# Four blocks of the first merge gate computed while the adaLN modulation is built, and the sample rows loaded as 128 contiguous half rows

## The chip, the cores and the metric

The kernel runs on one core of a Trainium2 chip. The metric is the device time of one execution in microseconds: 2131.4 us is the median of three runs of the kernel before (2131.13 to 2132.64). A core has TensorE (PE in the profile; its weight loads are PEld), VectorE (DVE), ScalarE (ACT), GpSimd (POOL) and SyncE (SP, which here issues most DMAs). They run on their own instruction streams, each in program order, and wait for each other by semaphores.

## The reference

The reference is one inference step of a one-layer hybrid decoder on 256 prompt tokens and 8 x 8 sample tokens (320 columns together), D_MODEL 2048, float32:

```
mod = silu(c) @ w_ada + b_ada;  shift, scale, gate = split(mod, 3)
h = rms_norm(x, pre_norm_g) * (1 + scale) + shift
(a_qkv, a_z, a_b, a_a, b_q, b_k, b_v, b_z, i_q, i_k, i_w, g_a, g_b) = split_columns(h @ w_in)
y_a, s_new, conv_new = gdn_branch(a_qkv, a_z, a_b, a_a, ...)      # gated DeltaNet
y_b = attend(q, k, v, i_q, i_w, i_k) * silu(b_z)                  # indexer picks top-k keys, sparse attention
merged = sigmoid(g_a) * (y_a @ w_pa) + sigmoid(g_b) * (y_b @ w_pb)
out = rms_norm(merged @ w_out, post_norm_g)
return x + gate * out, (k, v, i_k, s_new, conv_new)
```

What matters here is the first gate g_a: 2048 columns of w_in, that is 16 blocks of 128 features, each a product of a 2048 x 128 weight block with the 320 columns of h, followed by a sigmoid.

## The kernel before, in words

**The products.** Activations are kept with features on the partitions: xh and xl are a rounded high part and the rest of h, 16 blocks of 128 features by 320 tokens. A weight tile is split in the same way into whi (ACT copies it) and wlo (DVE subtracts), and a product is three matmuls: whi with xh, whi with xl, wlo with xh. A block of 128 output features over all 2048 input features takes 16 x 3 = 48 matmuls of 320 columns.

**The opening** (`startup`). h doesn't exist yet: each of its 16 feature blocks needs its shift and scale, which are columns of c @ w_ada. The opening goes in eight rounds q. In a round four tiles of w_ada of 1 MB (`columns`, four calls of eight matmuls each, fp32, listed as `pm<-raw,cT` or `rawx,cT`) give the modulation of two feature blocks; `operands` then turns the sum into columns (the `sel` matmuls, once a round), scales x and writes two blocks of xh and xl. As soon as these two blocks exist, the products that can use them run as jobs from a first-in first-out list (`fifo`, taken by `run(n)`): eight blocks of the indexer's queries (`iq_job`, EARLY = 8; 192 prompt and 64 sample columns), one block of values (`bv_job`), and five small blocks (`held_job`). The held ones keep a PSUM bank each for all rounds; the others write to a bank that is added to SBUF by DVE after each job (`add_to`) and goes back to the ring. That ring, `ps_main`, has three banks here (pm_65, pm_66, ps_72 in the listings), of which a round's `columns` hold one. The loads of a round (four tiles of w_ada, one of 1 MB for the queries, one of 0.72 MB for the small blocks) are issued by SP in the order of `seq`, as tiles of a ring of six come free. `split` makes awh and awl of the small blocks' weights; both have one buffer, so ACT can write awh only when the last held job of the round before has run.

**The stream.** Then 128-feature blocks are streamed through `stream`: two units of 24 matmuls a block, weights split two units ahead. Between the units (`side_round`) generators put in the instructions of the side work: attention of the prompt, the indexer's top-k, and `sample_branch`, which goes through eight samples b one after the other: bias and score matmuls, reductions on DVE, exponentials on ACT, transposes, copies, the product with V. A planner with a clock of its own decides at which unit a side step is put into the instruction streams. The chunks of the attention stage are, in order: the other eight query blocks, 16 blocks of b_q, 16 of b_z, 16 of g_a, and four early blocks of a_z. The next stage (DeltaNet) may only begin when every side generator has ended: `chunks[0].ready = lambda: not self.sides`. `stream` then calls `force`, which steps the side generators with no unit in between until they have all ended.

Of the kernel before, what the change touches and what calls it, by code (L numbers as in the profile page):

```python
# [17 lines left out]
NP = 256  # L18
# [17 lines left out]
EARLY = 8  # L36
AHEAD = 4
# [167 lines left out]
class Kernel:  # L205
# [210 lines left out]
    def build(self):  # L416
# [28 lines left out]
        for t in self.cst.free:  # L445
            self.nc.gpsimd.memset(t, 0.0)
# [18 lines left out]
    def consts(self):  # L465
# [6 lines left out]
        self.ident_b = self.l0.tile([128, 128], BF, name="ident_b")  # L472
        v.tensor_copy(self.ident_b, self.ident)
# [19 lines left out]
    def startup(self):  # L493
# [12 lines left out]
        awl = sp.tile([128, 2, 720], F32R, name="awl")  # L506
        seq = []
        for q in range(8):
            seq += [("a", q, 0), ("a", q, 1), ("a", 8 + q, 0), ("a", 8 + q, 1), ("i", q, 0), ("w", q, 0)]
        raws, aws, iqs = {}, {}, {}  # L510
        pos = {"n": 0}

        def load():
            while pos["n"] < len(seq):
                kind, q, h = seq[pos["n"]]
                r = awr if kind == "w" else ring
# [8 lines left out]
                elif kind == "w":  # L525
                    for d0, c0, n in ((0, C_IK, 144), (144, C_BA, 64), (208, C_BK, 512)):
                        nc.sync.dma_start(t[:, :, d0:d0 + n], w[rows, c0:c0 + n].rearrange("(k p) c -> p k c", p=128))
                    aws[q] = t
                else:
# [15 lines left out]
        for e in range(2):  # L545
            nc.scalar.dma_start(x[2][64 * e:64 * e + 64], xs[:, 1024 * e:1024 * e + 1024])
# [44 lines left out]
        both = sp.tile([128, 128], F32, name="both")  # L591
        for e in range(2):
            self.tt(both[:, 64 * e:64 * e + 64], self.ident[:, 0:64], self.ident[:, 64:128], OP.add)
# [23 lines left out]
        msb = sp.tile([128, 512], F32, name="msb")  # L617
# [14 lines left out]
        def split_i(q, g):  # L632
# [13 lines left out]
            low()  # L646

# [48 lines left out]

        def first_jobs():
# [8 lines left out]
        def jobs(q):  # L706
# [4 lines left out]
            fifo.append(lambda: bv_job(q))  # L711
            for j in range(len(held)):
                fifo.append(lambda j=j: held_job(q, j))
# [13 lines left out]
        def operands(q, turned=None):  # L727
# [3 lines left out]
            for e in range(4):  # L731
                self.mm(p[:, 9 * e:9 * e + 9], msb[:, 128 * e:128 * e + 128], self.sel)
# [16 lines left out]
        for q in range(8):  # L749
# [14 lines left out]
            if q == 1:  # L764
                run(2)
                split(0)
                run(2)
            p = self.ps_main.get()
            columns(q, 0, 0, p)
            if q == 0:  # L770
                idle_turns(14)
            columns(q, 0, 1, p)
            if q == 0:
                idle_turns(14)
            elif q == 1:
                run(4)
            else:
                split(q - 1)
                run(5)
# [3 lines left out]
            if q == 0:  # L783
# [5 lines left out]
                idle_turns(8)  # L789
            columns(q, 1, 1, p)  # L790
            self.act(msb, p)
# [4 lines left out]
            elif q > 1:  # L796
                run(4)
# [10 lines left out]
        jobs(7)  # L808
        run(5)
        split(7)  # L810
        run(4)
        self.split_ahead(1)
        run(3)
        self.split_ahead(2)
        run(2)
        self.ps_main.free.remove(self.side5)
        self.ps_side.put(self.side5)
        self.shut("start")
# [92 lines left out]
    def modulate(self, k, p, gs, mod, h):  # L911
        self.ts(h[:, :NP], p[:, :NP], gs[:, k, 0:1], mod[:, k, 0:1], OP.mult, OP.add)
        hs = h[:, NP:NT].rearrange("p (b t) -> p b t", t=TS)
        c0 = NP + 64 * (k // 8)
# [1532 lines left out]
```

## Time and profile before

| what | value |
|---|---|
| median of three runs | 2131.4 us |
| profiled execution, its own time | 2132.65 us |
| its span, first to last instruction | 2130.9 us |
| PE busy in the span | 2099.3 us (99%) |
| DVE, ACT, POOL busy | 66%, 46%, 22% |
| opening, first to last held job | until 169.6 us |
| attention stage, first to last streamed block | 169.7 to 715.7 us |
| `sample_branch`, K and V loop of eight samples | 561.9 to 715.7 us |

The page gives busy time by engine, then the span in 40 slices, then DMA queues, the chain of waits, and groups of instructions. Every operation goes through one helper, so all lines read L63 and instructions are told apart by tile names. Neighbouring matmuls overlap, so that the row of one shows 0.31 us while the next begins 0.147 us later: what a matmul costs is the distance between starts.

### The profile page before, as it was taken

The numbers are of one execution on the slowest core, as the hardware profiler recorded it, in microseconds if no ns is written. First come the engines' busy times: TensorE is split into PE (matmuls) and PEld (weight loads), VectorE is DVE, ScalarE is ACT, GpSimd is POOL, SyncE is SP. The second block draws the span as 40 slices with busy tenths as digits, with TensorE's granted clock in tenths as the row PEclk, the third lists the DMA queues.
The fourth block names the chain that finished last, engine by engine and source line by source line (L and its number), as shares of the span: only waits on it lengthen the run. The fifth ranks groups of instructions, "written<-read, shape, count | busy, mean of one in ns | idle before, by whom it ended". The sixth has DMA issues, their size and how long they took to land.

```text
span 2130.9 us, 43963 instructions
## 1 busy us (share of the span) xinstructions
PE 2099.3 (99%) x17055; PEld 2006.3 (94%) x17055; DVE 1410.9 (66%) x2881; ACT 989.6 (46%) x2257; POOL 463.1 (22%) x653
## 2 busy tenths in 40 slices
PE   7999999999999999999999999999999999999997
PEld 5889999899999999999999999999999999999997
DVE  4665657899755678868787878787746545445543
ACT  3235464333344455565656565656535424233343
POOL 2000100000001036545444444445440000000000
PEclk9999999999999999999999999999999999999999
DMA  9996656985787766777877777777787967555562
GB/s 332 355 309 173 181 151 178 289 256 151 201 238 239 205 181 173 211 210 207 207 200 199 208 196 210 193 212 192 200 218 210 268 180 218 161 155 146 166 178 85
DMA packets 720336, 438.91 MB, mean 206 GB/s; under 512 B 74144, under 2 KB 705536, under 8 KB 717824
## 3 DMA queue, kind: packets, MB, share of 16 engines
q1 hardware_dynamic: 716032, 413.45, 68.9%
q0 software_dynamic: 3616, 21.02, 3.0%
q8 instruction: 134, 2.20, 0.4%
q10 hardware_dynamic: 480, 1.65, 0.3%
q14 instruction: 74, 0.61, 0.1%
HBM read 386.81 MB, written 48.94 MB: 204 GB/s over the span
## 4 chain that ended last, share of the span: by engine, by line
PE 72%; issue 23%; DMA 2%; DVE 2%; ACT 0%; SPq 0%; DVEq 0%; POOL 0%; POOLq 0%; ACTq 0%
PE pm L63 56%; PE ps L63 16%; DMA raw<-in_w_ada_dram 1%; DVE S L63 1%; DMA rawx<-in_w_in_dram 1%; DVE wlo L63 0%; SPq L63 0%; DMA c<-in_c_sample_dram 0%; DVE awl L63 0%; DMA out_dram<-S 0%; ACT whi L63 0%; ACT ot L63 0%; DVE sga L63 0%; DVE w L63 0%; DVEq L2443 0%
## 5 line engine op out<-in xcount | busy, mean ns | idle before, releaser
L63 PE MATMUL pm<-xh,whi 128*128 128x320 f32 (+1 forms) x3284 | 996.1, 317 | 1.9 <-DVE qiS L63 0.8
L63 PE MATMUL pm<-xl,whi 128*128 128x320 f32 (+1 forms) x3284 | 962.1, 307 | 0.4 <-DVE xl L63 0.3
L63 DVE TENSOR_TENSOR wlo<-raw,whi 128x1024 fp32r<-128x1024 f32 x474 | 589.1, 1252 | 280.8 <-ACT whi L63 264.9
L63 PEld LDWEIGHTS pm<-xh,whi 128*128 128x128 f32 x3284 | 617.6, 188 | 32.2 <-issue 23.9
L63 PEld LDWEIGHTS pm<-xl,whi 128*128 128x128 f32 x3284 | 618.1, 188 | 1.7 <-DVE xl L63 0.8
L63 ACT ACTIVATE whi<-raw 128x1024 fp32r<-128x1024 f32 x474 | 497.7, 1058 | 169.7 <-PE pm L63 150.8
L63 PE MATMUL pm<-xh,wlo 128*128 128x320 f32 (+1 forms) x3284 | 547.6, 307 | 0.0
L63 PEld LDWEIGHTS pm<-xh,wlo 128*128 128x128 f32 x3284 | 495.4, 188 | 0.0
L63 POOL TENSOR_TENSOR X<-X,tmpx 48x31 f32<-48x31 f32 (+15 forms) x248 | 175.9, 709 | 19.4
L63 POOL TENSOR_TENSOR tmpx<-blk,X 48x31 f32<-48x31 f32 (+15 forms) x248 | 160.4, 647 | 51.0 <-DMA blk<-d_b 32.8
L63 PE MATMUL pm<-y1h,whi 128*128 128x320 f32 x512 | 151.3, 308 | 1.1 <-ACT y1h L63 1.1
L63 PE MATMUL pm<-y1l,whi 128*128 128x320 f32 x512 | 151.3, 307 | 0.2
L63 DVE SCALAR_TENSOR_TENSOR ps<-xp,cs,ps 128x344 f32<-128x344 f32 x192 | 111.5, 581 | 6.8
L63 POOL TENSOR_TENSOR rfin<-rfin,mh 128x3 f32<-128x3 f32 x1 | 0.8, 848 | 486.4 <-DVE rfin L63 486.4
L63 POOL TENSOR_TENSOR sc<-sc,mh 128x6 f32<-128x6 f32 (+1 forms) x24 | 43.6, 1815 | 277.0 <-DVE sc L63 213.0
L63 PEld LDWEIGHTS pm<-y1h,whi 128*128 128x128 f32 x512 | 95.7, 187 | 1.4 <-ACT y1h L63 1.3
L63 PEld LDWEIGHTS pm<-y1l,whi 128*128 128x128 f32 x512 | 96.1, 188 | 0.7 <-DVE y1l L63 0.7
L63 PE MATMUL pm<-y1h,wlo 128*128 128x320 f32 x512 | 85.4, 308 | 0.0
L63 PEld LDWEIGHTS pm<-y1h,wlo 128*128 128x128 f32 x512 | 77.7, 187 | 0.0
L63 DVE SCALAR_TENSOR_TENSOR S<-S,gtr,ps 128x128 f32<-128x128 f32 x256 | 67.4, 341 | 0.1
L63 ACT ACTIVATE xp<-pm 128x256 f32<-128x256 f32 (+1 forms) x128 | 32.0, 304 | 69.9 <-PE pm L63 69.9
L63 ACT ACTIVATE ot<-ot,sc 128x128 f32<-128x128 f32 x96 | 29.9, 390 | 72.3 <-DVE sc L63 72.3
(374 smaller groups left out, 2308.0 us busy)
## 6 DMA issues: line engine op xcount, KB each, us to landing
raw<-in_w_in_dram SPq DMA_DIRECT2D x336, 512.0 KB
raw<-in_w_pa_dram SPq DMA_DIRECT2D x64, 512.0 KB
rawx<-in_w_ada_dram SPq DMA_DIRECT2D x18, 1024.0 KB
a<-in_w_ada_dram SPq DMA_DIRECT2D x16, 1024.0 KB
S<-in_state_gdn_dram SPq DMA_DIRECT2D x32, 512.0 KB
out_dram<-S SPq DMA_DIRECT2D x32, 512.0 KB
raw<-in_w_pb_dram SPq DMA_DIRECT2D x32, 512.0 KB
raw<-in_w_out_dram SPq DMA_DIRECT2D x32, 512.0 KB
```

Of the source, the lines that this page charges most:

```text
L63: made = fn(*args, **kw)
```

## The change

Four of the sixteen g_a blocks (GATED = 4) leave the stream and become jobs of the opening. Each round loads two more row blocks of w_in by 512 columns (0.5 MB) into a single buffer gwr, listed in `seq` behind the round's other loads; `split_g` makes their high and low parts in the third pair of whi and wlo buffers; four `ga_job`s per round run 6 matmuls of 320 columns each and add the result into four SBUF tiles (two of them borrowed: auxf and vtok). In the last round the sums get their tanh, the affine step of the sigmoid, and the store to `d_siga`. In `startup` the jobs are also run in another pattern: before, the two `columns` calls of a half round stood together; now two or more jobs stand between all four. The modulation sums are evacuated into two 256-column tiles (`cst`, which the DeltaNet stage uses later, and whose clearing moves to the opening's end) in place of one of 512. A bf16 copy of the identity that nothing used is gone. The 64 sample rows of 2048 are loaded as 128 rows of 1024 (half rows, two to a token, next to each other) by one DMA in place of two, and `both` and `modulate` read them in that order.

```diff
 EARLY = 8
+GATED = 4
 AHEAD = 4
...
         self.cst = Ring([c.tile([128, 256], F32, name=f"cst{j}") for j in range(2)])
-        for t in self.cst.free:
-            self.nc.gpsimd.memset(t, 0.0)
         self.CS, self.CSV = {}, {}
...
         v.tensor_scalar(self.ident, ji, 0.0, None, op0=OP.is_equal)
-        self.ident_b = self.l0.tile([128, 128], BF, name="ident_b")
-        v.tensor_copy(self.ident_b, self.ident)
         self.ones = self.l0.tile([128, 128], F32, name="ones")
...
         awl = sp.tile([128, 2, 720], F32R, name="awl")
+        gwr = Ring([sp.tile([128, 2, 128 * GATED], F32, name="gwr")])
+        ga = [self.auxf[:, 0:NT], self.vtok.rearrange("p c d -> p (c d)")[:, 0:NT]]
+        ga += [sp.tile([128, NT], F32, name=f"ga{j}") for j in range(GATED - 2)]
         seq = []
         for q in range(8):
-            seq += [("a", q, 0), ("a", q, 1), ("a", 8 + q, 0), ("a", 8 + q, 1), ("i", q, 0), ("w", q, 0)]
-        raws, aws, iqs = {}, {}, {}
+            seq += [("a", q, 0), ("a", q, 1), ("a", 8 + q, 0), ("a", 8 + q, 1), ("i", q, 0), ("w", q, 0), ("g", q, 0)]
+        raws, aws, iqs, gws = {}, {}, {}, {}
         pos = {"n": 0}
...
                 kind, q, h = seq[pos["n"]]
-                r = awr if kind == "w" else ring
+                r = {"w": awr, "g": gwr}.get(kind, ring)
                 if not r.free:
...
                     aws[q] = t
+                elif kind == "g":
+                    nc.sync.dma_start(t, w[rows, C_GA:C_GA + 128 * GATED].rearrange("(k p) c -> p k c", p=128))
+                    gws[q] = t
                 else:
...
         xs = i["x_sample"].rearrange("b t d -> (b t) d")
-        for e in range(2):
-            nc.scalar.dma_start(x[2][64 * e:64 * e + 64], xs[:, 1024 * e:1024 * e + 1024])
+        nc.scalar.dma_start(x[2], xs.rearrange("r (e c) -> (r e) c", e=2))
         nc.scalar.dma_start(x[1], i["x_prompt"][0, 128:256, :])
...
         both = sp.tile([128, 128], F32, name="both")
+        pairs = lambda t: t.rearrange("p (r e) -> p r e", e=2)
         for e in range(2):
-            self.tt(both[:, 64 * e:64 * e + 64], self.ident[:, 0:64], self.ident[:, 64:128], OP.add)
+            self.tt(pairs(both)[:, :, e], pairs(self.ident)[:, :, 0], pairs(self.ident)[:, :, 1], OP.add)
 
...
         gs = sp.tile([128, KB, 9], F32, name="gs")
-        msb = sp.tile([128, 512], F32, name="msb")
+        msb = self.cst.free
         hT = [sp.tile([128, NT], F32, name=f"hT{j}") for j in range(2)]
...
             low()
+
+        def split_g(q):
+            r = gws.pop(q)
+            hi, lo = self.whi.get(), self.wlo.get()
+            hv, lv = (x.rearrange("p k c -> p (k c)").rearrange("p (k c) -> p k c", k=2) for x in (hi, lo))
+            halves[q, 2] = hi, lo, hv, lv
+            self.act(hv[:, :, :128 * GATED], r)
+            self.tt(lv[:, :, :128 * GATED], r, hv[:, :, :128 * GATED], OP.subtract)
+            gwr.put(r)
+            load()
 
...
 
+        def ga_job(q, j):
+            hi, lo, hv, lv = halves[q, 2]
+            p = self.ps_main.get()
+            products(q, p[:, :NT], hv, lv, 128 * j, 128, True, True)
+            add_to(q, p, [(ga[j], p[:, :NT])])
+            if j == GATED - 1:
+                self.whi.put(hi)
+                self.wlo.put(lo)
+                del halves[q, 2]
+            if q == 7:
+                t = ga[j]
+                self.act(t, t, AF.Tanh, scale=0.5)
+                self.ts(t, t, 0.5, 0.5, OP.mult, OP.add)
+                nc.sync.dma_start(self.d_siga[j], t)
+
         def first_jobs():
...
             fifo.append(lambda: bv_job(q))
+            for j in range(GATED):
+                fifo.append(lambda j=j: ga_job(q, j))
             for j in range(len(held)):
...
             for e in range(4):
-                self.mm(p[:, 9 * e:9 * e + 9], msb[:, 128 * e:128 * e + 128], self.sel)
+                self.mm(p[:, 9 * e:9 * e + 9], msb[e // 2][:, 128 * (e % 2):128 * (e % 2) + 128], self.sel)
             if q == 0:
...
                 run(2)
+            elif q > 1:
+                split(q - 1)
+                run(2)
             p = self.ps_main.get()
...
                 idle_turns(14)
+            else:
+                run(2)
+                if q == 1:
+                    split_g(0)
             columns(q, 0, 1, p)
...
             elif q == 1:
-                run(4)
+                run(2)
             else:
-                split(q - 1)
-                run(5)
+                run(3)
+                split_g(q - 1)
             if q >= AHEAD:
...
                 idle_turns(8)
+            else:
+                run(2)
             columns(q, 1, 1, p)
-            self.act(msb, p)
+            for e in range(2):
+                self.act(msb[e], p[:, 256 * e:256 * e + 256])
             self.ps_main.put(p)
...
                 idle_turns(5)
-            elif q > 1:
-                run(4)
+            else:
+                run(1 if q == 1 else 4)
             if q in then:
...
         jobs(7)
+        split(7)
         run(5)
-        split(7)
+        split_g(7)
         run(4)
         self.split_ahead(1)
-        run(3)
+        run(4)
         self.split_ahead(2)
-        run(2)
+        run(5)
         self.ps_main.free.remove(self.side5)
         self.ps_side.put(self.side5)
+        for t in self.cst.free:
+            nc.gpsimd.memset(t, 0.0)
         self.shut("start")
...
         hs = h[:, NP:NT].rearrange("p (b t) -> p b t", t=TS)
-        c0 = NP + 64 * (k // 8)
         bc = lambda a: a[:, k, 1:9].rearrange("p (b o) -> p b o", o=1).to_broadcast([128, NB, TS])
-        self.tt(hs, p[:, c0:c0 + 64].rearrange("p (b t) -> p b t", t=TS), bc(gs), OP.mult)
+        self.tt(hs, p[:, NP:384].rearrange("p (b t e) -> p e b t", t=TS, e=2)[:, k // 8], bc(gs), OP.mult)
         self.tt(hs, hs, bc(mod), OP.add)
...
         chunks += self.pairs(w, C_BZ, 16, self.bz_done, r)
-        ga = self.pairs(w, C_GA, 16, lambda p, h: self.gate_done(p, h, self.d_siga, self.t_r), r)
+        ga = self.pairs(w, C_GA + 128 * GATED, 16 - GATED,
+                        lambda p, h: self.gate_done(p, GATED + h, self.d_siga, self.t_r), r)
         ga[0].before = lambda: self.spawn(self.conv_gen(0))
```

The first place where instructions move is PE's stream in the fifth round of the opening (q = 4), behind the last of the held jobs that the round begins with (ps_71 is its accumulator). Before:

```order
L63 MATMUL ps_71<-xh,awl 128x320 x2
L63 MATMUL pm_65<-rawx_165,cT 32x256 x8
L63 MATMUL pm_65<-raw_75,cT 32x256 x8
L63 MATMUL pm_66<-xh,whi_78 128x256
L63 MATMUL pm_66<-xl,whi_78 128x256
L63 MATMUL pm_66<-xh,whi_78 128x256
```

and with the change:

```order
L64 MATMUL ps_72<-xh,whi_78 128x256
L64 MATMUL ps_72<-xl,whi_78 128x256
L64 MATMUL ps_72<-xh,whi_78 128x256
L64 MATMUL ps_72<-xl,whi_78 128x256
L64 MATMUL ps_72<-xh,wlo_81 128x256 x2
L64 MATMUL pm_66<-xh,whi_78 128x256
L64 MATMUL pm_66<-xl,whi_78 128x256
L64 MATMUL pm_66<-xh,whi_78 128x256
L64 MATMUL pm_66<-xl,whi_78 128x256
L64 MATMUL pm_66<-xh,wlo_81 128x256 x2
L64 MATMUL pm_65<-rawx_161,cT 32x256 x8
L64 MATMUL ps_72<-xh,whi_78 128x256
```

Two query jobs have moved ahead of the first `columns`, and the third job (last row, bank ps_72 again) follows it where the second `columns` stood. On DVE the subtraction of awl still stands ahead of the additions that free these banks; with the change, in the same round:

```order
L64 TENSOR_TENSOR awl<-awr_163,awh 128x1440
L64 TENSOR_TENSOR q_137<-ps_72,q_137 128x192
L64 TENSOR_TENSOR qiS<-ps_72,qiS 128x8x8
L64 TENSOR_TENSOR q_138<-pm_66,q_138 128x192
L64 TENSOR_TENSOR qiS<-pm_66,qiS 128x8x8
```

The second place is PE at the sixth sample of `sample_branch` (its product with V is the row `a,a`, `vS` belongs to it; `esel` and `bs` are the bias matmuls of the next sample). Before, with the units of the stream around it:

```order
L63 MATMUL ps_67<-a_1770,a_1773 64x128 x16
L63 MATMUL ps_67<-vS,a_1773 64x128 x2
L63 MATMUL pm_66<-xh,whi_78 128x320
L63 MATMUL pm_66<-xl,whi_78 128x320
```

and with the change:

```order
L64 MATMUL ps_69<-a_2038,a_2039 64x128 x16
L64 MATMUL ps_69<-vS,a_2039 64x128 x2
L64 LDWEIGHTS esel
L64 MATMUL ps_67<-bs,esel 128x256
L64 LDWEIGHTS esel
L64 MATMUL ps_70<-bs,esel 128x256
```

From here on no matmul of the stream follows until the eighth sample is done; the next one stands here:

```order
L64 MATMUL ps_69<-a_2036,a_2039 64x128 x16
L64 MATMUL ps_69<-vS,a_2039 64x128 x2
L64 MATMUL ps_71<-ident,a_2040 128x128
L64 MATMUL pm_65<-xh,whi_79 128x320
L64 MATMUL pm_65<-xl,whi_79 128x320
```

Before, 168 matmuls of the stream stand between the sixth sample's product with V and the end of the eighth; with the change none does. The stream has 192 fewer to place.

The third place is SP's queue for the opening's second round (q = 1), where the new load stands between the small blocks' weights and the first tile of w_ada of the next round. Before:

```order
L63 DMA awr_167<-in_w_in_dram 128x2x512
L63 DMA raw_76<-in_w_ada_dram 128x8x256
```

and with the change:

```order
L64 DMA awr_163<-in_w_in_dram 128x2x512
L64 DMA gwr<-in_w_in_dram 128x2x512
L64 DMA raw_76<-in_w_ada_dram 128x8x256
```

What is behind gwr on SP waits until `split_g` has emptied that one buffer.

## Prediction

> **What bounds the kernel now.** I read the page first, then the waits of PE, then single stretches of the timeline. Busy time by engine and the share of it in 40 slices (a digit is tenths):
>
> ```profile
> span 2130.9 us, 43963 instructions
> PE 2099.3 (99%) x17055; PEld 2006.3 (94%) x17055; DVE 1410.9 (66%) x2881; ACT 989.6 (46%) x2257; POOL 463.1 (22%) x653
> ...
> PE   7999999999999999999999999999999999999997
> ```
>
> PE works all the time; 31.6 us of the span are without it. Work that moves from one place on PE to another is worth nothing by itself: the change can only win where PE waits in the opening, and it loses wherever the removed work was cover for something else. So two questions decide: how much PE waits in the opening, and what stood behind the four blocks in the stream.
>
> The waits of PE from 30 to 171 us (total, times, longest):
>
> ```profile
> PE pm L63 <- DMA raw<-in_w_ada_dram: 2.2, 2, 1.8
> PE pm L63 <- DVE qiS L63: 2.0, 4, 1.2
> PE pm L63 <- ACT msb L63: 0.7, 1, 0.7
> ```
>
> The rounds can be told by the `sel` matmuls, eight listed rows once a round; the first, two neighbours, and the eighth:
>
> ```profile
> 27.12 1.06 PE L63 MATMUL pm<-sel,msb 128*128 128x9 f32 x8
> ...
> 100.22 1.06 PE L63 MATMUL ps<-sel,msb 128*128 128x9 f32 x8
> ...
> 117.36 1.06 PE L63 MATMUL pm<-sel,msb 128*128 128x9 f32 x8
> ...
> 151.74 1.06 PE L63 MATMUL pm<-sel,msb 128*128 128x9 f32 x8
> ```
>
> Seven rounds take 124.6 us. A round without a wait takes 17.14 (100.22 to 117.36), seven of them 120.0: only 4.6 us of waits are there to be filled. DMA is as full as PE in this stretch (30 to 150 us):
>
> ```profile
> DMA packets 38358, 42.40 MB, mean 353 GB/s; under 512 B 3003, under 2 KB 34761, under 8 KB 38345
> ```
>
> That is 6.05 MB in 17.1 us; opening rounds are bound by both at once.
>
> **The change part by part.**
>
> *The work that moves.* A matmul of 320 columns costs the distance between starts; these two rows are 12 matmuls apart:
>
> ```profile
> 689.68 0.31 PE L63 MATMUL pm<-xh,whi 128*128 128x320 f32 x1
> ...
> 691.44 0.31 PE L63 MATMUL pm<-xh,whi 128*128 128x320 f32 x1
> ```
>
> 0.147 us. Four blocks are 192 matmuls, 28.2 us less in the stream; the opening gets the same 192, 3.5 us a round for eight rounds. The moved loads: 0.52 MB more a round, 6.57 MB at 353 GB/s is 18.6 us, against 17.14 + 3.5 = 20.7 us of PE. From the second or third round on PE is the later one, so the DMA waits of 2.2 us go. The single gwr holds back the next round's w_ada tiles on SP until mid round; they then have about 15 us of PE work ahead of them and their first tile needs (0.5 + 1) MB, under 5 us: hidden. If that cover were gone, every us would be paid seven times. The split of the new weights (ACT, DVE) and the additions (DVE) lie beside PE, which has 3.5 us of work for them each round; where they get in its way is the third part.
>
> *What the four blocks covered.* After the change nothing of the stream is left beside the last samples of `sample_branch`; the DeltaNet stage waits for them. One sample's chain, from its predecessor's product with V on, all engines:
>
> ```profile
> 676.68 1.97 PE L63 MATMUL ps<-a,a 128*64 128x128 f32 x32
> ...
> 678.93 0.94 POOL L63 DMA_INDIRECT a<-in_cache_k_dram,idx  x1 [14.30 <-PE ps L63]
> ...
> 680.90 0.31 PE L63 MATMUL ps<-bs,esel 32*128 32x256 bf16 x5
> ...
> 683.12 1.42 DVE L63 TENSOR_REDUCE st<-ps 128x1 f32<-128x256 f32 x4 [1.10 <-PE ps L63]
> ...
> 684.77 0.32 ACT L63 ACTIVATE a<-ps,st 128x64 f32<-128x64 f32 x1 [4.35 <-DVE st L63]
> ...
> 686.78 0.22 ACT L63 ACTIVATION_READ_ACCUMULATOR a<-ps,st 128x1 f32 x1
> ...
> 688.19 2.37 DVE L63 STREAM_TRANSPOSE a<-a 128x1024 f32<-128x1024 f32 x2
> ...
> 688.63 0.92 PE L63 MATMUL ps<-ident,a 32*128 32x32 f32 x33
> ...
> 691.78 0.93 DVE L63 COPY a<-ps 128x256 f32<-128x256 f32 x3
> ...
> 715.74 0.39 PE L63 MATMUL pm<-xh,whi 128*128 128x320 f32 x1
> ```
>
> The last row is the first matmul of the DeltaNet stage. The gather's time to landing is in the view of tile a (min/median/max):
>
> ```profile
> DMA to landing us min/median/max: 7.6/8.1/9.7
> ```
>
> Today the stretch from 676.68 (sixth sample's product with V) to 715.74 takes 39.1 us: 168 stream matmuls, 24.7, and 14.4 of the samples' own PE work. There is no slack: the samples end where the stream does. Uncovered, I add the chain: product with V 2.3 (to 678.93); seventh sample's bias and scores 2.2; maxima 1.65; exponentials 2.2, at 8.4. The next K, asked for at 2.3, lands 8.1 later, at 10.4; DVE's transposes 2.4 and, queued behind them, its copies 0.9 end at 13.7; product with V 2.3, at 16. The eighth: 2.2 + 1.65 + 2.2, PE transposes 0.9, copies 1.0, product 2.3, output 0.6, at 26.9; with some 0.1 us at each of six handovers 27.5. Another 24 matmuls (3.5 us) are gone just ahead. So the attention stage gets shorter by 39.1 - 27.5 + 3.5 = 15.1 us, and not by 28.2: **+13.1 us**. Bounds: with no wait for K 25.9, with the slowest gather 29.1, so +11.5 to +14.7.
>
> *The new pattern in the opening.* Two `columns` calls together, one alone, and the border between them and the jobs:
>
> ```profile
> 52.86 1.07 PE L63 MATMUL pm<-raw,cT 128*32 128x256 f32 x16 [1.84 <-DMA raw<-in_w_ada_dram]
> 53.86 0.38 PE L63 MATMUL pm<-xh,whi 128*128 128x256 f32 x1
> ```
>
> ```profile
> 105.27 0.45 PE L63 MATMUL ps<-xh,awl 128*128 128x320 f32 x2
> 105.52 1.40 ACT L63 ACTIVATE awh<-awr 128x1440 fp32r<-128x1440 f32 x1 [0.46 <-ACT whi L63]
> 105.65 1.93 PE L63 MATMUL ps<-rawx,cT 128*32 128x256 f32 x32
> ...
> 106.95 1.66 DVE L63 TENSOR_TENSOR awl<-awr,awh 128x1440 fp32r<-128x1440 f32 x1 [0.64 <-ACT awh L63]
> 107.52 0.39 PE L63 MATMUL pm<-xh,whi 128*128 128x256 f32 x1
> 107.74 0.28 PE L63 MATMUL pm<-xl,whi 128*128 128x256 f32 x1
> 107.86 0.28 PE L63 MATMUL pm<-xh,whi 128*128 128x256 f32 x1
> ...
> 108.54 0.36 DVE L63 TENSOR_TENSOR q<-pm,q 128x192 f32<-128x192 f32 x1
> 108.81 0.21 DVE L63 TENSOR_TENSOR qiS<-pm,qiS 128x64 f32<-128x64 f32 x1
> ...
> 109.08 0.39 PE L63 MATMUL pm<-xh,whi 128*128 128x256 f32 x1
> ```
>
> One call alone lasts 1.00 (52.86 to 53.86), two together 1.87 (105.65 to 107.52). The first job matmul behind them takes 0.22 in place of 0.12, the two ahead 0.38 in place of 0.29. Two calls apart cost 2 x 1.00 - 1.87 + 0.19 = 0.32 us more than together. The change parts both pairs in seven rounds: 14 x 0.32 = **+4.5 us**.
>
> Then the banks. awl of a round starts when ACT has awh, and ACT waits for the last held job (105.52); DVE has awl at 108.6 and only then frees the banks of the first query jobs: the third starts at 109.08, at the very moment its bank is free. Two `columns` calls now fill that time. With the change the first two jobs (0.72 each) and one call (1.2 with its borders) end at 108.3, and the third job stands 0.8 us for its bank. It and everything behind it on PE wait. In rounds 2 to 4 both halves of the query weights are split ahead of awl, and PE waits there already today (0.4 to 0.5 each of the 2.0 us above): 1.2. In round 1 the one call taken out of the way costs 0.5. Together 3 x 0.8 + 3 x 1.2 + 0.5 = **+6.5 us**; nothing if I have misread the bank (lower bound), 9 if DVE's added split delays more.
>
> *The rest.* In the opening's tail the wait for awl only moves from one job to another, and the tanh chain on ACT and DVE ends beside the held jobs, 4.4 us of PE: I take +0.5 for its start. Two evacuations for one are covered by the four gate jobs, in round 0 +0.1. The sample rows: the same 512 KB of 4 KB pieces; PE's first work waits for w_ada, not for them: 0, between -0.5 and +0.5. The clearing of `cst` and the dropped identity stood at a time when PE had nothing to do: 0.
>
> *Sum.* +13.1 - 4.6 + 4.5 + 6.5 + 0.6 = **+20.1 us**. On the profiled execution: span 2130.9 + 20.1 = 2151.0, and 1.75 around it (2132.65 against its span) is 2152.8; this execution lies 1.25 over the median of the runs, so **2151.5 us**.
>
> **The rivals.**
>
> *A: only the lost cover counts.* The banks come free in time and PE doesn't notice the new pattern: +13.1 + 0.6, with 4.6 gained or lost, 2140 to 2149, say 2145. For it, DVE is busy for 13 of 20 us only (the columns are PE, PEld, DVE, ACT, POOL, clock, DMA share, GB/s):
>
> ```profile
> 100.00:120.00 20.00, 20.00 (x185) 17.29 (x184) 13.06 (x40) 5.02 (x7) 0.00 (x0) 1.00 1.09 356
> ```
>
> Against it, awl's place in DVE's order hasn't moved.
>
> *B: PE's clock falls in the uncovered stretch.* The chain above leaves PE idle three times for about 4 us (for the seventh sample's softmax, its copies, the eighth's softmax). At the end of the trace the granted clock falls soon after PE stops:
>
> ```profile
> 2118.00:2121.00 3.00, 1.29 (x11) 1.03 (x11) 1.34 (x3) 0.62 (x4) 0.85 (x1) 0.96 0.00 0
> 2121.00:2131.00 10.00, 0.00 (x0) 0.00 (x0) 5.11 (x5) 0.00 (x0) 0.00 (x0) 0.50 0.73 262
> ```
>
> (The column ahead of the last two is the clock, 1.00 elsewhere.) If it falls in each gap, PE's 8 us behind them on the chain take up to twice as long, less what recovers, and the stream's first matmuls too: +5 to +9, 2158. The Trainium skill, "TensorE: Matmul & The Clock Gate", section "HAM oscillation — how this bites in real kernels", warns of PE-idle gaps over about 3.4 us; by its free-running windows a gap of 4 us holds a whole one only now and then. The trace agrees that the clock halves (0.50); that 4 us are enough no row here shows, so it stays a rival.
>
> *C: faster.* PE's rows overlap, so busy may hide slack; if the opening's rounds go by bytes alone, they grow by 0.52 MB each, 1.5 us, 12 in all, and with 15.1 saved in the stream the kernel is 3 us faster: 2128. It decides from the point at which the opening grows by less than 15.1 us. Against it: from 100 to 150 us starts follow each other without a wait, 17.14 us of PE in a round of 17.14. The Trainium skill, "Perfetto Trace Analysis", section "Identifying the Most-Contended Engine", holds matmul busy to be no good measure and LDWEIGHTS busy the better one; by it PE would have 2.7 of 20 us to spare here (17.29). But the fp32 calls load only 32 columns each, which lowers that share without any pause.
>
> *D: the one gwr starves PE.* Loads start late in each round and PE waits at `columns`: 2 us a round, +14 more, 2166. Against it: 15 us of lead.
>
> **How the numbers follow.** The sum 0.57, A 0.17, B 0.16, C 0.06, D 0.04. The time is that of the sum, 2151.5. The range reaches into A below (no bank waits, cheap handovers: 2140) and B above (2163). A difference under 0.2%, 4.3 us, can't be told from none. Faster by more has half of C, 0.03; the same the rest of C and a little of A, 0.05; slower 0.92.
>
> **What would show it.** The attention stage should end with some 27 us in which PE is half busy and no `whi` row stands (five tenths in the windows); in the opening, rounds of about 22 us in place of 17.14, DMA below full, and a PE wait on DVE qiS of about 1 us in each. Wrong would be: no such stretch, rounds under 20.7, or waits on gwr or w_ada from the third round on.

## The result, and the profile after

2151.3 us, the median of four runs (2151.05 to 2153.7), against 2131.8 before (2131.13 to 2132.64): a ratio of 1.0093, with a 95% interval from 1.0079 to 1.0107. The change makes the kernel slower by 19.5 us; 20.1 were forecast. The head of the page after:

```profile
span 2149.7 us, 44005 instructions
...
PE 2108.1 (98%) x17055; PEld 2010.5 (94%) x17055; DVE 1419.8 (66%) x2908; ACT 991.5 (46%) x2269; POOL 462.5 (22%) x653
...
PE   8999999999999899999999999999999999999997
```

PE has the same 17055 matmuls; the 8 in slice 14 of 40 (699 to 752 us) is new, in the middle of a kernel of nines. To see where 18.8 us of span come from I cut both traces at the same two instructions: the first transpose of auxf on PE, which ends the opening, and the first copy of a DeltaNet block out of PSUM (xp on ACT), which ends the attention stage. Before, PE's timeline, then the view of tile xp (min/median/max in ns, then the first and the last start in us):

```profile
170.97 0.37 PE L63 MATMUL ps<-ident,auxf 80*128 80x80 f32 x3
```

```profile
L63 ACT ACTIVATE xp<-pm x34: 220/318/396, 723.1 to 890.7; 128x256 f32<-128x256 f32 x17, 128x64 f32<-128x64 f32 x17
```

After:

```profile
205.04 0.37 PE L64 MATMUL ps<-ident,auxf 80*128 80x80 f32 x3
```

```profile
L64 ACT ACTIVATE xp<-pm x30: 222/306/387, 742.8 to 886.4; 128x256 f32<-128x256 f32 x15, 128x64 f32<-128x64 f32 x15
```

The opening grows by 34.1 us for 28.2 us of work; the attention stage shrinks from 552.1 to 537.8, by 14.4 for the same 28.2; the rest of the program takes 1406.9 in place of 1407.8. The sum is 18.8.

**The opening after.** The fourth, fifth, sixth and eighth `sel` marks, and PE's waits from 28 to 210 us:

```profile
92.66 1.06 PE L64 MATMUL ps<-sel,cst 128*128 128x9 f32 x8
...
115.17 1.06 PE L64 MATMUL pm<-sel,cst 128*128 128x9 f32 x8
...
137.26 1.06 PE L64 MATMUL ps<-sel,cst 128*128 128x9 f32 x8
...
181.43 1.06 PE L64 MATMUL pm<-sel,cst 128*128 128x9 f32 x8
```

```profile
PE pm L64 <- DVE qiS L64: 5.0, 6, 1.3
PE ps L64 <- DVE qiS L64: 3.3, 4, 1.1
```

From the fourth mark on a round takes 22.1 to 22.5 us in place of 17.14. The waits for DMA are gone, and every round from the second on has one wait of 0.7 to 1.1 us on qiS; the longest, 1.3, lies in the tail behind the rounds. This is the sixth round, PE and DVE:

```profile
121.90 1.66 DVE L64 TENSOR_TENSOR awl<-awr,awh 128x1440 fp32r<-128x1440 f32 x1 [0.64 <-ACT awh L64]
...
122.03 1.07 PE L64 MATMUL pm<-rawx,cT 128*32 128x256 f32 x16
123.48 0.35 DVE L64 TENSOR_TENSOR q<-pm,q 128x192 f32<-128x192 f32 x1
123.74 0.21 DVE L64 TENSOR_TENSOR qiS<-pm,qiS 128x64 f32<-128x64 f32 x1
...
124.01 0.39 PE L64 MATMUL pm<-xh,whi 128*128 128x256 f32 x1 [0.92 <-DVE qiS L64]
```

PE has done two jobs and one `columns` call when the third job needs a bank whose addition stands behind awl on DVE.

**The uncovered stretch after.** PE's timeline from the sixth sample's product with V to the first DeltaNet matmul, then windows over the wait for the seventh sample's softmax and what follows it (the column behind the five engines is the granted clock):

```profile
707.23 1.97 PE L64 MATMUL ps<-a,a 128*64 128x128 f32 x32
...
715.65 0.92 PE L64 MATMUL ps<-ident,a 32*128 32x32 f32 x33 [3.44 <-ACT a L64]
718.86 4.02 PE L64 MATMUL ps<-a,a 128*64 128x128 f32 x32 [2.29 <-issue]
...
729.71 1.01 PE L64 MATMUL ps<-ident,a 32*128 32x32 f32 x33 [3.74 <-ACT a L64]
730.98 3.50 PE L64 MATMUL ps<-a,a 128*64 128x128 f32 x32 [0.27 <-ACT a L64]
...
735.45 0.39 PE L64 MATMUL pm<-xh,whi 128*128 128x320 f32 x1
```

```profile
712.20:715.60 3.40, 0.01 (x1) 0.00 (x0) 1.10 (x4) 2.23 (x10) 1.46 (x7) 1.00 0.98 382
715.60:718.80 3.20, 0.92 (x33) 0.69 (x33) 3.14 (x7) 0.66 (x2) 0.00 (x0) 0.68 0.52 215
718.80:722.90 4.10, 4.04 (x34) 3.65 (x36) 0.48 (x2) 0.00 (x0) 0.00 (x0) 0.50 0.01 4
```

For 28.2 us (707.23 to 735.45) there is no row of the stream. Behind each long wait for a softmax the clock is halved, and the next product with V takes 4.0 and 3.5 us. At full clock it takes 1.97, or 2.31 where no stream stands beside it (the kernel with matmuls in the gaps, below).

### The profile page after: what moved, and what is told of

It reads as the page before. It is cut to its first block, busy times and chain, and to the rows that moved or that the text cites. A ratio compares the mean times of both kernels' runs of the same rounds, so it can differ in the third digit from the quotient of the medians.

```text
span 2149.7 us, 44005 instructions
## 1 busy us (share of the span) xinstructions
PE 2108.1 (98%) x17055; PEld 2010.5 (94%) x17055; DVE 1419.8 (66%) x2908; ACT 991.5 (46%) x2269; POOL 462.5 (22%) x653
## 4 chain that ended last, share of the span: by engine, by line
PE 41%; issue 23%; DVE 2%; ACT 0%; DMA 0%; DVEq 0%; POOL 0%; POOLq 0%; SPq 0%; ACTq 0%
PE pm L64 33%; PE ps L64 8%; DVE S L64 1%; DVE wlo L64 0%; DMA out_dram<-S 0%; DVE w L64 0%; DVE ps L64 0%; ACT ot L64 0%; ACT a L64 0%; DVE sga L64 0%; DVEq L2486 0%; ACT whi L64 0%; DVE sc L64 0%; POOL sc L64 0%; DVE ot L64 0%
## 5 line engine op out<-in xcount | busy, mean ns | idle before, releaser
L64 DVE TENSOR_TENSOR wlo<-raw,whi 128x1024 fp32r<-128x1024 f32 x466 | 576.8, 1247 | 265.5 <-ACT whi L64 252.9
L64 ACT ACTIVATE whi<-raw 128x1024 fp32r<-128x1024 f32 x466 | 489.4, 1058 | 174.6 <-PE pm L64 151.4
```

Of the source, the lines that this page charges most:

```text
L64: made = fn(*args, **kw)
```

## The experiments

Each is timed beside the kernel before on the same chip. The time is the median of all executions, and ratios carry their 95% intervals; stages are cut as above, in the one execution that was profiled.

| kernel | time, us | against before | opening | attention stage | rest |
|---|---|---|---|---|---|
| before | 2131.8 to 2132.9 | 1 | 171.0 | 552.1 | 1407.8 |
| changed | 2151.3 | 1.0093 (1.0079 to 1.0107) | 205.0 | 537.8 | 1406.9 |
| additions first | 2148.1 | 1.0077 (1.0060 to 1.0094) | 199.1 | 538.7 | 1408.6 |
| columns paired | 2145.9 | 1.0069 (1.0052 to 1.0085) | 196.5 | 540.6 | 1407.9 |
| more cover | 2162.1 | 1.0143 (1.0126 to 1.0160) | 204.5 | 552.1 | 1403.7 |
| transposes in the gaps | 2150.2 | 1.0085 (1.0068 to 1.0102) | 204.6 | 537.3 | 1406.4 |
| matmuls in the gaps | 2148.3 | 1.0072 (1.0057 to 1.0088) | 204.6 | 535.3 | 1407.2 |
| paced | 2144.0 | 1.0059 (1.0043 to 1.0074) | 204.8 | 526.8 | 1408.2 |
| paired, late split, paced | 2140.9 | 1.0036 (1.0023 to 1.0050) | 202.4 | 528.3 | 1409.3 |
| paired and covered | 2130.3 | 0.9986 (0.9977 to 0.9995) | 196.8 | 523.9 | 1407.2 |
| before, rows only | 2130.5 | 0.9990 (0.9981 to 0.9999) | 169.1 | 552.1 | 1407.6 |
| before, rows in two loads | 2132.9 | 0.9999 (0.9990 to 1.0008) | 171.6 | 552.1 | 1407.8 |

The rest of the program varies between 1406.4 and 1409.3 with no edit there (more cover apart); differences of a us or two in it are not explained below.

### Bank waits: the additions first

```diff
             elif q > 1:
-                split(q - 1)
                 run(2)
+                split(q - 1)
```

> The changed kernel (2151.3 us) with one swap: in rounds 2 to 7 the first two query jobs stand ahead of the split of the small blocks' weights, so that on DVE the additions that free two banks come before the subtraction of awl. Theory of the prediction (PE waits for banks because awl stands ahead of them): the waits of PE on DVE qiS, 8.3 us in the changed kernel, fall to about 2, and the time by about 6, to 2145. In rounds 2 to 4 both halves of the query weights still stand ahead on DVE; if these are what is late there, only 3 us come back, 2148. Rival (DVE as a whole is late, awl only sets which job pays for it): the wait moves to another job, 2151.

PE's waits for banks from 28 to 210 us:

```profile
PE pm L64 <- DVE qiS L64: 1.6, 2, 1.3
PE ps L64 <- DVE qiS L64: 1.6, 2, 1.1
```

8.3 us become 3.2, those of the second round and of the tail; in the rounds from the third on none is left. The opening ends 5.9 us sooner, of which 0.4 lies ahead of the first `sel` mark (25.33 against 25.71), where the edit changes nothing; in that execution the clock came up to full at 12.4 us, in the changed kernel's at 13.6. That is about the theory's 6: the waits come from the place of awl in DVE's order, and the halves of the query weights, which still stand ahead in rounds 2 to 4, aren't what is late. The time falls by 3.2 only. Of the difference 0.9 is in the attention stage, where this execution had more halved clock (a mean of 0.77 over its uncovered stretch of 29.2 us, 0.82 in the changed kernel), and 1.7 is in the rest, unexplained.

### Partings: the columns in pairs

```diff
             elif q > 1:
                 split(q - 1)
-                run(2)
             p = self.ps_main.get()
             columns(q, 0, 0, p)
             if q == 0:
                 idle_turns(14)
-            else:
-                run(2)
-                if q == 1:
-                    split_g(0)
             columns(q, 0, 1, p)
...
             elif q == 1:
                 run(2)
+                split_g(0)
+                run(2)
             else:
-                run(3)
+                run(7)
                 split_g(q - 1)
...
-            else:
-                run(2)
             columns(q, 1, 1, p)
...
-                run(1 if q == 1 else 4)
+                run(3 if q == 1 else 6)
```

> The changed kernel with the order of the opening as it was before: the two columns calls of a half round together, all jobs behind them (7 and 6 a round), the four gate blocks still in the opening. Theory of the prediction: 14 partings of 0.32 us (4.5) and the bank waits (6.3 above those of the kernel before) both go: 10.8 less, 2140.5, rounds of about 20.7 us. Rival A' (parting costs nothing, only the waits go): 6.3 less, 2145. Rival A (the pattern is free, the banks wait in either order): 2151. Rival (together, the columns wait for their tiles again, 2.2 and 0.7 us as in the kernel before): 2143 to 2144.

The fifth and the eighth mark with the columns in pairs, and then with the additions first (columns apart); in neither does PE wait for anything in these three rounds:

```profile
110.52 1.06 PE L64 MATMUL pm<-sel,cst 128*128 128x9 f32 x8
...
172.95 1.06 PE L64 MATMUL ps<-sel,cst 128*128 128x9 f32 x8
```

```profile
111.96 1.06 PE L64 MATMUL pm<-sel,cst 128*128 128x9 f32 x8
...
175.48 1.06 PE L64 MATMUL pm<-sel,cst 128*128 128x9 f32 x8
```

A round takes 20.81 us against 21.17: a parting costs 0.18 us, and not 0.32, which makes 2.5 for fourteen. The opening ends 8.5 us before that of the changed kernel (5.9 of waits, 2.6 of partings), and not 10.8. With 20.81 a round is 3.67 longer than a quick round before (17.14), for 3.5 of added matmuls: in pairs the moved work costs its own time. The whole gained only 5.5 at the median. The attention stage is 2.8 us longer than in the changed kernel, with more halved clock again (0.77 over the stretch of 29.6 us, and 0.81 over the 8.8 behind it), and the rest 1.0. By the time alone rival A' (2145) would fit; the opening shows that it doesn't.

### Cover: four other blocks in the place of the removed ones

```diff
-EARLY_Z = (0, 4)
+EARLY_Z = (0, 4, 8, 12)
```

> The changed kernel with four more blocks of a_z (192 matmuls, 28.2 us) taken out of the DeltaNet stage and streamed at the end of the attention stage, where the four gate blocks had stood; nothing else is changed. Theory (the lost cover of the last samples is a cost of its own): the stretch from the sixth sample's product with V to the first DeltaNet matmul is covered again as in the kernel before and ends no later than the stream; of the 28.2 us moved there 14 are hidden, and the time falls by 14, to 2137.5. Rival (the blocks are cover where they stand today, too, and the DeltaNet stage waits for its chains once they are gone): about 2151, or slower. If the samples move with the stream only in part: 2140 to 2145.

The attention stage takes 552.1 us, to a tenth what it took before. It was given 28.2 us of work over the changed kernel's 537.8, and only 14.3 of them show: half of what the stream puts there is free, as the samples are paced here. But the kernel is 10.8 slower and not 13.8 faster. The rest shrinks by 3.2 for 28.2 us taken out. Waits of PE in the DeltaNet stage (760 to 1520 us), first changed, then with more cover:

```profile
PE ps L64 <- DVE S L64: 1.1, 2, 0.6
```

```profile
PE pm L64 <- ACT whi L64: 6.7, 4, 2.2
PE ps L64 <- DVE vt L64: 4.0, 4, 1.6
PE pm L64 <- DVE wlo L64: 1.9, 4, 0.9
PE ps L64 <- DVE S L64: 1.8, 4, 0.6
```

The rival held: the a_z blocks are cover where they stand, too. Of the 25 us that are missing 13.3 are these waits. The clock was halved three times there, for 13.7 us together; with PE at work all that time this would be 6.8 us more (an estimate from the clock records), and the remainder stays open. So these blocks gave no cover for nothing; what was left to try was to move the side work.

### The clock: something for PE to do in the gaps

```diff
+            if b >= 6:
+                self.busy_turns(24)
...
+            if b == 6:
+                self.busy_turns(15)
             yield self.ready(pT, V[b])
```

The first call stands behind the loop that issues the exponentials. `busy_turns` writes to a free bank that nobody reads: transposes of the identity in the first kernel, in the second 22 and 14 products of xh with itself.

> The changed kernel with transposes of the identity that nobody reads put into PE's three gaps of the uncovered stretch: 24 (3.0 us) behind the scores of the seventh and of the eighth sample, 15 (1.9 us) ahead of the seventh's product with V. They lie in time in which PE waits for others. In the changed kernel the granted clock halves twice in this stretch, and the two products with V take 4.0 and 3.5 us in place of 1.97. Theory (the gaps lower the clock, and this costs 3.9 us): the clock stays at 1.00, the products take 2.0, the time falls by 3 to 4, to 2147.5. Rival (the clock falls for another reason, or the slow products lie beside another wait): no change, 2151; if the extra transposes get in the way, 2152 to 2153.

> The changed kernel with matmuls of 320 columns that nobody reads in PE's gaps of the uncovered stretch: 22 (3.2 us) behind the scores of the seventh and the eighth sample, 14 (2.1 us) ahead of the seventh's product with V; they take the places of the transposes of the run before this, in which the clock still halved once. Over four kernels the attention stage got longer by 0.32 us for each us of halved clock. Theory (the halved clock, 10.2 us of it in the changed kernel, costs 3.3 us): if it stays at 1.00, the attention stage takes 534.5 (537.76), the time is 2148. If it halves once more, as with transposes: 2150. Rival (the clock isn't what is slow there): 2151 with the clock at 1.00.

The uncovered stretch with transposes and with matmuls (windows):

```profile
706.80:733.00 26.20, 22.55 (x379) 18.44 (x379) 10.36 (x30) 7.92 (x30) 2.90 (x10) 0.94 0.37 128
```

```profile
706.80:732.60 25.80, 23.24 (x374) 19.28 (x374) 10.49 (x30) 7.87 (x30) 2.87 (x10) 1.00 0.39 129
```

The longest gap left in the stretch with transposes, the longest with matmuls, and a gap in "paired, late split, paced" (below), behind which the clock was halved as well:

```profile
727.21 0.92 PE L64 MATMUL ps<-ident,a 32*128 32x32 f32 x33 [1.06 <-ACT a L64]
```

```profile
719.28 2.31 PE L64 MATMUL ps<-a,a 128*64 128x128 f32 x32 [1.06 <-issue]
```

```profile
718.64 3.51 PE L64 MATMUL ps<-a,a 128*64 128x128 f32 x32 [2.27 <-ACT a L64]
```

With matmuls the clock stays at 1.00, the stretch takes 25.8 in place of 28.2 us, the attention stage 535.3 (534.5 expected), and the time falls by 3.0 (3.3 expected). So the halved clock costs about 2.5 us in the changed kernel. With transposes the clock was still halved once, for 6.8 us from 729.7 on, although the longest gap in the stretch was 1.06 us, as long as the longest with matmuls. The Trainium skill, "TensorE: Matmul & The Clock Gate", section "HAM oscillation — how this bites in real kernels", gives the rule of no PE-idle gap over about 3.4 us: the gaps of 3.44 and 3.74 above agree. The run with 1.06 doesn't, nor do the halvings behind gaps of at most 1.62 and 2.17 us (more cover) and 2.27 us (the row above): no gap of 3.4 us was needed. The Trainium skill, "TensorE: Matmul & The Clock Gate", section "Part 4: PE-mode transpose", says that transposes don't count as PE-busy in the same way. The runs don't bear this out. The clock was halved behind the second 24 transposes and not behind the first, and at the start of the kernel before, where PE runs 30 of the same transposes, they raise it by themselves:

```profile
8.39 4.91 PE L63 MATMUL ps<-ident 128*128 128x128 f32 x30
```

They start 0.21 us apart until the clock record goes to full at 11.33, and 0.11 us apart from then on. Why the clock halved with transposes in the gaps and not with matmuls stays open; the matmuls also filled 0.5 to 0.7 us more of each gap.

### Cover again: the same work, the samples sooner

```diff
-            yield self.ready(pT, V[b])
+            yield self.ready(pT, V[b]) - 2.0
```

> The changed kernel with one edit: in the loop over the samples the step of the product with V is offered 2.0 us sooner by the planner's clock; a sample takes 72 matmuls of the stream in place of 96, and the eighth ends 36 ahead of the stream's end. Same work, nothing moved. Theory (the 13.8 us by which the attention stage got less shorter than its work are lost cover): they come back, 2137.5, no halved clock, PE above 99% busy until the DeltaNet stage. Rival (the samples at that pace wait for K, V or copies, and PE with them): 2140 to 2145. Rival (something else in the stage is slower): 2151.

The attention stage takes 526.8 us: 10.9 of the 13.8 come back without one instruction moved between stages. My count of the last sample was wrong: the seventh, not the eighth, ends 36 matmuls ahead of the stream's end. PE's waits for the eighth are what is left, 210 to 750 us:

```profile
PE ps L64 <- ACT a L64: 2.8, 2, 2.3
```

In the profiled execution (2141.6) the clock stayed at 1.00; the median of four runs is 2144.0, up to 2147.2. The time goes with the mean granted clock of the whole execution: 2141.6 at 0.998 and 2147.2 at 0.995 here, 2144.6 at 0.995 and 2151.3 at 0.993 with pairs alone. So by these means the halved clock differs from one execution of a kernel to the next.

### Together, in two tries

Both have the columns in pairs and the product with V offered 2.0 us sooner. The first also put the split behind two jobs, as in the first experiment; against the kernel with pairs:

```diff
-            elif q > 1:
-                split(q - 1)
             p = self.ps_main.get()
...
             else:
-                run(7)
+                run(2)
+                split(q - 1)
+                run(5)
                 split_g(q - 1)
...
+        run(2)
         split(7)
-        run(5)
+        run(3)
```

> The changed kernel with three edits: columns calls in pairs, as in the kernel before; the split of the small blocks' weights two jobs later, in the tail too; and in the loop over the samples the step of the product with V is offered 2.0 us sooner by the planner's clock, so that a sample takes three units of the stream (72 matmuls) in place of four and the eighth ends 36 matmuls ahead of the stream's end. Theory: the opening ends at 195 (205.04 in the changed kernel, 196.52 with pairs alone), the attention stage takes the 552.1 of the kernel before less 28.2, the rest 1407.5: span 2126.8, time 2128.5, 0.17% faster than the kernel before. Rival (the quicker pace makes PE wait for gathers or copies, 0.5 to 1 us a sample): 2132 to 2136. Rival (the stage's cover isn't what is missing): 2143.

The time is 2140.9 and not the 2128.5 expected. The opening ends at 202.4 and not at 195; the attention stage takes 528.3 in place of 523.9, with 2.8 us of PE's waits for the eighth sample, as in the paced kernel, and 3.4 us of halved clock. DVE in the sixth round:

```profile
122.36 0.21 DVE L64 TENSOR_TENSOR qiS<-ps,qiS 128x64 f32<-128x64 f32 x1
122.49 1.65 DVE L64 TENSOR_TENSOR awl<-awr,awh 128x1440 fp32r<-128x1440 f32 x1
124.06 0.35 DVE L64 TENSOR_TENSOR q<-pm,q 128x192 f32<-128x192 f32 x1
124.33 0.21 DVE L64 TENSOR_TENSOR qiS<-pm,qiS 128x64 f32<-128x64 f32 x1
```

awl now lies between the second and the third job's additions, and with no `columns` behind the jobs to give DVE time PE waits 1.08 us in every round from the third on. awl costs next to nothing (0.27 us in two rounds of the kernel with pairs) where PE has `columns` beside it: behind two jobs when these stand ahead of a call, ahead of all jobs when the two calls stand first. The second try leaves the split where pairs alone had it, and lets the samples' top-k start its steps sooner:

```diff
             nc.vector.match_replace(self.scs, m8[:64], self.scs, TAKEN)
-            yield self.clock.last - 1.8
+            yield self.clock.last - 2.6
```

> The changed kernel with the columns calls in pairs (the split of the small blocks' weights back ahead of them) and the samples moved ahead: the product with V offered 2.0 us sooner, each of the 32 steps of the sample's top-k 2.6 us sooner in place of 1.8. In program order all eight products with V now stand 72 matmuls of the stream apart, the eighth at its end. Theory: the opening ends at 196.5, as with pairs alone; the stage takes 524 (552.1 of the kernel before less 28.2) and PE's 2.8 us of waits for the eighth sample go; the rest takes 1407.5: span 2128, time 2130, 0.1% faster than the kernel before, no halved clock. Rival (the top-k's reductions on DVE can't be had sooner, and PE waits for them in the loop's first samples): 2133 to 2137.

The time is 2130.3, 0.9986 of the kernel before (0.9977 to 0.9995). The stage ends at the row below and takes 523.9 us, 552.1 less 28.2 to a tenth; PE waits 0.5 us in all of it, as in the kernel before, and the clock stays at 1.00:

```profile
L64 ACT ACTIVATE xp<-pm x36: 221/317/396, 720.7 to 898.5; 128x256 f32<-128x256 f32 x18, 128x64 f32<-128x64 f32 x18
```

So what the change lost in the attention stage was cover, with the halved clock as a part of its price. But this kernel isn't faster than the next one, which has no gate blocks in the opening at all.

### The sample rows alone

```diff
-        for e in range(2):
-            nc.scalar.dma_start(x[2][64 * e:64 * e + 64], xs[:, 1024 * e:1024 * e + 1024])
+        nc.scalar.dma_start(x[2], xs.rearrange("r (e c) -> (r e) c", e=2))
```

in the kernel before, with the two places that read them; and then the same rows in the same order by two loads:

```diff
-        nc.scalar.dma_start(x[2], xs.rearrange("r (e c) -> (r e) c", e=2))
+        xr = xs.rearrange("r (e c) -> (r e) c", e=2)
+        for e in range(2):
+            nc.scalar.dma_start(x[2][64 * e:64 * e + 64], xr[64 * e:64 * e + 64])
```

> The kernel before with the sample rows of the change alone (one load of 128 contiguous half rows in place of two of 64 rows, and the two places that read them). The prediction took 0 for it, between -0.5 and +0.5: 2132. The trace of the changed kernel speaks for more: its first round's fourth columns call starts at 23.86 in place of 25.34 us and the sel matmuls at 25.71 in place of 27.12, and each of SP's first three tiles of w_ada is issued sooner. Theory S (the new shape of the load frees the tiles' way): 1.4 to 1.8 us less, 2130.5, first sel at about 25.5. Rival (the head start comes from the clearing of cst and the identity that were dropped): sel at 27.1, 2132.

> The kernel before with the sample rows in the new order of 128 half rows, but loaded by two DMAs of 64 contiguous half rows each. With the one load of 128 rows the time fell by 1.8 us: the 128 pieces of 4 KB took 0.169 us each on the queue, 0.286 in the kernel before. Theory H (64 partitions at a time are what is slow): 0.28 us a piece, first sel at 27, 2132. Theory R (rows of 4 KB with a gap of 4 KB between them are what is slow): 0.17, sel at 25.3, 2130.5.

What DMA moved from 4 to 12 us: before, rows in one load, rows in two loads.

```profile
DMA packets 1182, 2.41 MB, mean 302 GB/s; under 512 B 97, under 2 KB 921, under 8 KB 1049
```

```profile
DMA packets 1563, 3.10 MB, mean 387 GB/s; under 512 B 158, under 2 KB 1251, under 8 KB 1379
```

```profile
DMA packets 1141, 2.46 MB, mean 307 GB/s; under 512 B 104, under 2 KB 866, under 8 KB 994
```

One load: 0.69 MB more in the same 8 us, 1.8 us at 387 GB/s. The 128 pieces of 4 KB took 0.169 us each in the trace (0.286 before), the first sel comes at 25.21 (27.12 before), the time is 2130.5, 0.9990 of the kernel before (0.9981 to 0.9999). Two loads of contiguous rows: 0.253 us a piece, sel at 27.28, nothing gained. So the two loads of 64 partitions are what was slow, and the gaps between the rows were little of it. In the ten kernels with one load the first sel comes at 25.15 to 25.71, in the two with two loads at 27.12 and 27.28. No run parts the number of loads from the partitions that each reaches (two loads of half rows over all 128 partitions would). The Trainium skill, "SBUF — State Buffer", section "Can I just issue two DMAs to hit both halves?", says that only one transfer over all 128 partitions reaches all SBUF ports and that two over halves don't add up. These runs agree: 307 GB/s with two such loads, 387 with one.

## Why the prediction was right, step by step

**The opening: +35.2 forecast, +34.1 measured.** Through the runs it comes apart as 28.2 for the work, -1.9 for the sample rows (171.0 to 169.1 with them alone), -0.8 for waits that the new work fills (196.5 with pairs, against 169.1 + 28.2), +2.6 for the partings, +5.9 for the banks (5.5 from the first mark on).

- *Bank waits, +6.5:* right, 5.9, by the mechanism given. The share of rounds 2 to 4 (q = 2 to 4) was misjudged: the prediction read waits of 0.4 to 0.5 us there before and added them, 1.2 a round. The four waits of that row were 0.29, 0.26, 0.26 and 1.18, the last in the tail; after the change the wait in these rounds is 0.89, and in the three behind them 0.70 to 0.92.
- *Partings, +4.5:* right in kind, the size off: 0.18 us each in place of 0.32.
- *Waits filled, -4.6:* wrong. I took all that the seven rounds lasted over the quickest as time to be filled. In the kernel with pairs 2.6 us of waits on qiS remain (2.4 before), in the first rounds and the tail; what more work fills are the 2.2 on DMA and the 0.7 on msb, and by the marks only 0.8 is gained. In the seven rounds alone it is 1.7 (22.9 us longer for 24.6 of work, from the first to the eighth mark), but the tail takes 0.8 more than its work.
- *Sample rows, 0:* wrong, -1.9, and outside of the bounds of half a us. The step looked at bytes and pieces, which are the same; what changed is that one load over 128 partitions stands in place of two over 64.

The two errors of the last points are of opposite sign (3.8 too much gained, 1.9 too little), and the partings' 1.9 too much nearly closes the sum. That it came out within 1.1 us is luck.

**The attention stage: -15.1 forecast, -14.4 measured.** Lost cover was the largest term, and the paced kernels show it: with the same work the stage falls to 523.9. The chain was forecast at 27.5 and took 28.2, but by another road. The wait for the eighth K (1.6 of the 27.5) didn't come: DVE's transposes of it began 6.6 us after the gather was issued, where I had taken 8.1:

```profile
709.49 0.94 POOL L64 DMA_INDIRECT a<-in_cache_k_dram,idx  x1 [10.78 <-PE ps L64]
...
716.09 2.36 DVE L64 STREAM_TRANSPOSE a<-a 128x1024 f32<-128x1024 f32 x2
```

At full clock the chain is 25.8, my own figure "with no wait for K 25.9". The 2.5 us on top are rival B's, which the sum had at nothing. That the two errors partly cancel is luck: with the 1.6 us for K as well the time would be near 2153 (an estimate, 2151.3 + 1.6).

**The rivals.** B happened behind two of the three gaps that it names, the waits for a softmax; behind the third, of 2.29 us, the clock was halved already. Its price was half: 2.5 us for 5 to 9, since the clock came back to 1.00 ahead of the stream's first matmuls and the scores. A falls by the bank waits that went with one swap. C falls with the rounds: 22 us, with DMA below full (303 GB/s from 50 to 150 us, 353 before). D falls with the waits: none on gwr or w_ada from the third round on. What "What would show it" named was there, but PE was busy for 18.0 of the 28.2 us, more than half. The rest of the program was taken as unchanged; its -0.9 us lies within what it varies by.

## What to carry to other kernels

Work taken out of a stream saves its time only if nothing latency-bound beside it (a chain of steps that each wait for the one before) needs the cover: cut the trace at the ends of the stages, and set the change of each stage against the work moved. Where cover is lost, pacing the side work can get it back for nothing (all 13.8 us here), while other work moved in can uncover the place that it came from (25 us here). An instruction between a matmul and the addition that frees its bank belongs where PE has work without a bank to wait for; the place that is right in one pattern is wrong in another.

## What the hardware showed that I hadn't expected

- Two loads of 64 partitions held up the other loads on the DMA engines: 302 GB/s in place of 387 over 8 us, for 512 KB of the same pieces, with the engines busy all the time.
- PE's clock halved in a stretch whose longest gap was 1.06 us (filled with transposes), and didn't with matmuls there; yet at the kernel's start such transposes alone raised it to full. A halved piece lasted 3.4 us or a multiple of it in the clock records of the traces (3.41, 6.83). One kernel's time spread by 6.7 us with it (columns paired, 2144.6 to 2151.3).
- At full clock, beside no stream, a product with V took 2.31 us in place of 1.97 (in the kernel with matmuls in the gaps and in the paced one); the runs do not say why.
